# One TensorE-bound kernel, one core: the constants' tiles allocated in another order

## The chip, the core and the metric

The kernel runs on one core of one Trainium2 chip. The time is device microseconds of one execution; the median of three runs counts. A core has TensorE (PE in the profile, its weight loads apart as PEld), VectorE (DVE), ScalarE (ACT), GpSimd (POOL) and SyncE (SP), which here issues all transfers. All tiles of SBUF have an address in bytes within a partition; "at a multiple of 256" below is said of that address.

## What is computed

Two layers of an encoder on 256 frames of 1,024 channels in float32. Each layer normalises its input, projects it by one wide matrix, lets three token mixers work on slices of the projection, merges them by gates, and adds an output projection to its input. Cut to what matters here:

```python
for l in range(DEPTH):                       # 2
    h = _rms(x, norm_g[l])                   # 256 x 1024
    proj = h @ w_in[l]                       # 1024 x 9304
    (gq, gk, gv, ga, gz, bq, bk, bv, iq, ik, iw, bz,
     cq, ck, cv, cz, gate) = jnp.split(proj, SPLIT_AT, axis=-1)
    ...
    merged = (g[:, :, 0] * (y_a @ w_br[l, 0])
              + g[:, :, 1] * (y_b @ w_br[l, 1])
              + g[:, :, 2] * (y_c @ w_br[l, 2]))
    x = x + merged @ w_out[l]
```

## The kernel before

Every float32 operand of a large product is split into a rounded high part and the rest, and a product is three matmuls: high by high, high by low, low by high. `mm3` issues them (lines 183, 184 and 185), so each line of the profile with one of these numbers is one of the three. Each matmul loads its own stationary operand.

The input of a layer is normalised, transposed on TensorE and written by `norm_in` into two tiles, `hTh` (high) and `hTl` (low), each 128 partitions by 8 blocks of channels by 256 frames; line 224 (ACT) writes the high part and line 225 (DVE) the low part. They stay in place for both layers. A slice of them for a block k and a half t of the frames is 128 columns, 512 bytes of each partition, and slices follow each other every 512 bytes.

Weights come in units of 512 KB, laid out on the host in the order of use. For each unit `Stream.need` issues the transfer into a `raw` tile, ACT writes the high part `whi` and DVE the low part `wlo` (line 145). There are 5 `raw` tiles and 6 of each of the others, and units are asked for 21 ahead.

The large matmuls are of three kinds.

- 16 projections of 512 columns in a layer (`bq`, `cq`, `ck`, `cz`, `bk`, `cv`, `gq`, `bv`, `gv`, `gz`, and `gate` six times), through `proj` and `project`. The slice of `hTh` or `hTl` is stationary and 512 columns of `whi` or `wlo` stream past it. A projection has 4 units of 2 blocks, 2 halves and 3 matmuls, so 48 matmuls; in two layers they are 32 x 48 = 1,536.
- `iq` and `bz`, through `project_T`: here 128 columns of the weights are stationary and `hTh[:, k]` or `hTl[:, k]`, 256 columns, stream; 96 matmuls each in a layer, 384 in all. `small_task` has 24 more such in a layer.
- The branch projections `br` and the output projection `out`, again with 512 columns of the weights streaming (at the very end some with 256). Their stationary slices are those of `yTh`, `yTl`, `ybh`, `ybl`, `mTh` and `mTl`, which lie in the pool's tag `kp`.

Between them `Flow.pump` lets smaller tasks issue their matmuls at fixed points of the program; the order of every engine is settled when the program is built, by a scheduler's model, and doesn't depend on the run.

The pool `cp` holds what stays for the whole run. It hands out addresses in the order in which its tiles are asked for: `x` (line 102), `eyeg` (109, the identity and the gains), `half`, `warm` (111, 112), `pk`, `wah`, `wal` (113 to 115), `hTh`, `hTl` (200, 201), and some small ones after these. The pool begins at byte 16,512, which is 128 above a multiple of 256. The pools of the weights and of the work tiles stand behind it: the 17 tiles of the weights' pool begin at 49,152 and all lie at multiples of 4,096, and the tiles of `kp` begin at 138,496 (541 times 256) and are 2,048 bytes each, so their slices of 512 bytes lie at multiples of 256 too.

Of the kernel before, what the change touches and what calls it, by code (L numbers as in the profile page):

```python
# [8 lines left out]
F32 = mybir.dt.float32  # L9
F32R = mybir.dt.float32r  # L10
# [6 lines left out]
L, T, D, BR = 2, 256, 1024, 512  # L17
NB = 3
P = 128
NOSYNC = mybir.DependencyInfo(mybir.DependencyClass.NoSync, mybir.DependencyReason.DATA)  # L20
CH = 512
KD8 = D // P
# [43 lines left out]
def trunk(ctx: ExitStack, tc: tile.TileContext, x_in, units, wsmall, eye, pack, ptmp, wa2b, out):  # L66
# [3 lines left out]
    cp = ctx.enter_context(tc.tile_pool(name="cp", bufs=1))  # L70
# [6 lines left out]
    def nm(s):  # L77
        cnt[0] += 1
        return f"{s}_{cnt[0]}"
# [19 lines left out]
    def at(shape, n="at"):  # L99
        return pp.tile(shape, F32, tag="at", bufs=4, name=nm(n))  # L100

    x = cp.tile([P, 2, D], F32, name="x")
    HV = [slice(h * 512, h * 512 + 512) for h in range(2)]

# [3 lines left out]

    eyeg = cp.tile([P, P + L * KD8], F32, name="eyeg")
    ident, gT = eyeg[:, :P], eyeg[:, P:]  # L110
    half = cp.tile([P, 16], F32, name="half")
    warm = cp.tile([P, 16], F32, name="warm")
    pk = cp.tile([P, NPK], F32, name="pk")
    wah = cp.tile([P, L, 256], F32R, name="wah")
    wal = cp.tile([P, L, 256], F32R, name="wal")
# [77 lines left out]
    def split(ps, shape, n, mk=None):  # L193
# [2 lines left out]
        A.activation(hi, ps, AF.Copy)  # L196
        V.tensor_sub(lo, ps, hi.bitcast(F32))
        return hi, lo

    hTh = cp.tile([P, KD8, T], F32R, name="hTh")  # L200
    hTl = cp.tile([P, KD8, T], F32R, name="hTl")

    ss = [cp.tile([P, 2], F32, name=f"ss{t}") for t in range(2)]

# [731 lines left out]
```

## Time and profile before

| what | value |
|---|---|
| median of three runs | 612.82 us (612.48 to 613.51) |
| the profiled execution | 613.26 us |
| its span, first to last instruction | 611.5 us |
| TensorE busy | 604.2 us, 99% of the span |
| VectorE, ScalarE, GpSimd busy | 434.1, 354.0, 63.0 us |
| mean granted clock of TensorE | 0.994 of full speed |
| read from memory | 99.23 MB, 164 GB/s over the span |

A page of the profile gives the busy time of each engine, the chain of work that ended last, and groups of instructions with their number and the mean length of one. Matmuls are pipelined and their ends are modelled, so in a stream their lengths overlap and are not what they cost. What a matmul costs in a stream is the distance from its start to the start of the next, called its pitch below; the timeline, with starts in hundredths of a microsecond, gives it, best as a mean over a long run.

### The profile page before, as it was taken

To read this page: it belongs to the slowest core of one execution; us is meant where nothing else is said; L and a number is where in the kernel's file an instruction comes from. 1 tells how busy PE (TensorE), PEld (TensorE's weight loads), DVE (VectorE), ACT (ScalarE), POOL (GpSimd) and SP (SyncE) were. 2 spreads that over 40 slices of the span, in tenths; PEclk is the share of its full clock that TensorE was granted. 3 is DMA by queue.
4 is the path that set the end of the run, shared out by engine and by line. 5 is a ranking of instruction groups with operands and counts; after the bars stand their busy time and mean duration, and the time that the engine had idled before them with its cause. 6 is when DMAs were issued, how large, how long until landed. Compare 5 with 4: busy or idle time off the path is not lost.

```text
span 611.5 us, 8711 instructions
## 1 busy us (share of the span) xinstructions
PE 604.2 (99%) x3180; PEld 507.3 (83%) x3180; DVE 434.1 (71%) x709; ACT 354.0 (58%) x612; POOL 63.0 (10%) x93
## 2 busy tenths in 40 slices
PE   7999999999999999999999999999999999999997
PEld 4788888898899888888878888889888988888886
DVE  5888657777989756648587776676888976575571
ACT  6778855766536754443466787576755555544430
POOL 2033101000022000000001340201000120000000
PEclk7999999999999999999999999999999999999999
DMA  8764565425534635555527455533554165455501
GB/s 319 279 208 138 173 206 173 138 104 173 173 103 167 190 129 198 177 194 181 172 87 244 152 161 183 195 115 104 184 167 166 48 230 158 152 177 201 178 30 70
DMA packets 28699, 100.85 MB, mean 165 GB/s; under 512 B 3184, under 2 KB 3696, under 8 KB 28656
## 3 DMA queue, kind: packets, MB, share of 16 engines
q1 hardware_dynamic: 28656, 100.30, 49.6%
q8 instruction: 25, 0.41, 0.3%
q14 instruction: 18, 0.15, 0.1%
HBM read 99.23 MB, written 1.05 MB: 164 GB/s over the span
## 4 chain that ended last, share of the span: by engine, by line
PE 97%; ACT 1%; DMA 1%; DVE 0%; SPq 0%; issue 0%
PE gate L183 7%; PE gate L184 7%; PE gate L185 7%; PE br L183 4%; PE br L184 4%; PE br L185 4%; PE out L185 2%; PE out L183 2%; PE out L184 2%; PE bz L185 1%; PE bz L183 1%; PE cq L183 1%; PE bz L184 1%; PE iq L183 1%; PE iq L185 1%; PE iq L184 1%
## 5 line engine op out<-in xcount | busy, mean ns | idle before, releaser
L145 DVE TENSOR_TENSOR wlo<-raw,whi 128x1024 fp32r<-128x1024 f32 x184 | 224.1, 1222 | 100.1 <-ACT whi L145 98.8
L145 ACT ACTIVATE whi<-raw 128x1024 fp32r<-128x1024 f32 x184 | 193.8, 1060 | 148.6 <-PE gate L185 39.6
L183 PE MATMUL gate<-whi,hTh 128*128 128x512 f32 x192 | 76.6, 399 | 0.0
L184 PE MATMUL gate<-wlo,hTh 128*128 128x512 f32 x192 | 76.1, 396 | 0.0
L185 PE MATMUL gate<-whi,hTl 128*128 128x512 f32 x192 | 75.9, 395 | 0.0
L185 PEld LDWEIGHTS gate<-whi,hTl 128*128 128x128 f32 x192 | 36.1, 188 | 8.1
L183 PEld LDWEIGHTS gate<-whi,hTh 128*128 128x128 f32 x192 | 36.1, 188 | 7.8
L184 PEld LDWEIGHTS gate<-wlo,hTh 128*128 128x128 f32 x192 | 36.2, 188 | 7.7
L190 POOL TENSOR_TENSOR r<-v,half 128x4 f32<-128x4 f32 (+1 forms) x24 | 34.2, 1424 | 2.0
L189 POOL TENSOR_SCALAR v<-ss 128x4 f32<-128x4 f32 (+1 forms) x24 | 11.8, 490 | 182.3 <-DVE ss L268 111.0
L183 PE MATMUL out<-whi,mTh 128*128 128x512 f32 (+1 forms) x72 | 26.7, 371 | 0.0
L184 PE MATMUL out<-wlo,mTh 128*128 128x512 f32 (+1 forms) x72 | 26.3, 366 | 0.0
L185 PE MATMUL out<-whi,mTl 128*128 128x512 f32 (+1 forms) x72 | 26.2, 366 | 0.0
L184 PE MATMUL br<-wlo,yTh 128*128 128x512 f32 x64 | 25.0, 390 | 0.0
L183 PE MATMUL br<-whi,yTh 128*128 128x512 f32 x64 | 25.0, 390 | 0.0
L185 PE MATMUL br<-whi,yTl 128*128 128x512 f32 x64 | 24.9, 389 | 0.0
L183 PE MATMUL iq<-hTh,whi 128*128 128x256 f32 x64 | 18.5, 289 | 0.0
L185 PE MATMUL bz<-hTh,wlo 128*128 128x256 f32 x64 | 18.2, 285 | 0.0
L184 PE MATMUL iq<-hTl,whi 128*128 128x256 f32 x64 | 18.2, 284 | 0.0
L183 PE MATMUL bz<-hTh,whi 128*128 128x256 f32 x64 | 18.1, 283 | 0.0
L184 PE MATMUL bz<-hTl,whi 128*128 128x256 f32 x64 | 18.0, 282 | 0.0
L185 PE MATMUL iq<-hTh,wlo 128*128 128x256 f32 x64 | 18.0, 281 | 0.0
(320 smaller groups left out, 1511.1 us busy)
## 6 DMA issues: line engine op xcount, KB each, us to landing
raw<-in_units SPq DMA_DIRECT2D x184, 512.0 KB, 3.4
x<-in_x SPq DMA_DIRECT2D x4, 256.0 KB, 4.5
wsr<-in_wsmall SPq DMA_DIRECT2D x2, 416.0 KB, 6.3
out<-x SPq DMA_DIRECT2D x3, 256.0 KB, 2.0
pt<-in_ptmp SPq DMA_DIRECT2D x1, 384.0 KB, 7.3
wa<-in_wa2b SPq DMA_DIRECT2D x1, 256.0 KB, 7.3
out<-x SPq DMA_DIRECT2D x2, 128.0 KB, 1.7
pk<-in_pack SPq DMA_DIRECT2D x1, 133.0 KB, 7.6
```

The lines of the kernel that those rows point to most:

```text
L145: self.splits.append((A.activation(hi, raw, AF.Copy), V.tensor_sub(lo, raw, hi.bitcast(F32))))
L183: TE.matmul(ps, lh, rh, start=first, stop=False)
L184: TE.matmul(ps, lh, rl, start=False, stop=False)
L185: TE.matmul(ps, ll, rh, start=False, stop=last)
L189: G.tensor_scalar(v, ss, 1.0 / dim, EPS, op0=OP.mult, op1=OP.add)
L190: G.tensor_tensor(r, v, half[:, :n], op=OP.pow)
```

## The change

The requests for `half`, `warm`, `hTh` and `hTl` are moved ahead of the one for `x`. Nothing else is edited. On each of the five engines the built program has the same instructions in the same order as before. What differs is where nine tiles lie:

| tile | bytes | address before | above a multiple of 256 | address after | above a multiple of 256 |
|---|---|---|---|---|---|
| `hTh` | 8,192 | 30,592 | 128 | 16,640 | 0 |
| `hTl` | 8,192 | 38,784 | 128 | 24,832 | 0 |
| `x` | 8,192 | 16,512 | 128 | 33,024 | 0 |
| `eyeg` | 576 | 24,704 | 128 | 41,216 | 0 |
| `half` | 64 | 25,280 | 192 | 16,512 | 128 |
| `warm` | 64 | 25,344 | 0 | 16,576 | 192 |
| `pk` | 1,064 | 25,408 | 64 | 41,792 | 64 |
| `wah` | 2,048 | 26,496 | 128 | 42,880 | 128 |
| `wal` | 2,048 | 28,544 | 128 | 44,928 | 128 |

All tiles behind these, those of the other pools included, keep their addresses. Slices of 512 bytes of `hTh` and `hTl` lie 384 bytes above a multiple of 512 before, and 256 above one after, as do the slices in `kp`.

```diff
+    half = cp.tile([P, 16], F32, name="half")
+    warm = cp.tile([P, 16], F32, name="warm")
+    hTh = cp.tile([P, KD8, T], F32R, name="hTh")
+    hTl = cp.tile([P, KD8, T], F32R, name="hTl")
     x = cp.tile([P, 2, D], F32, name="x")
...
     eyeg = cp.tile([P, P + L * KD8], F32, name="eyeg")
     ident, gT = eyeg[:, :P], eyeg[:, P:]
-    half = cp.tile([P, 16], F32, name="half")
-    warm = cp.tile([P, 16], F32, name="warm")
     pk = cp.tile([P, NPK], F32, name="pk")
...
-    hTh = cp.tile([P, KD8, T], F32R, name="hTh")
-    hTl = cp.tile([P, KD8, T], F32R, name="hTl")
```

## Rows read from the trace of the kernel before

**Rows 1.** The page, its first part (engine, busy us, share of the span, instructions) and the first line of its fourth (the chain that ended last, by engine).
```profile
PE 604.2 (99%) x3180; PEld 507.3 (83%) x3180; DVE 434.1 (71%) x709; ACT 354.0 (58%) x612; POOL 63.0 (10%) x93
...
PE 97%; ACT 1%; DMA 1%; DVE 0%; SPq 0%; issue 0%
```

**Rows 2.** The waits of TensorE over the whole span: who waited for whom, us in total, times, longest.
```profile
PE bq L183 <- ACT hTh L224: 1.3, 2, 1.1
...
PE cq L183 <- ACT whi L145: 0.3, 1, 0.3
PE bq L184 <- DVE wlo L145: 0.2, 1, 0.2
```

**Rows 3.** Groups of matmuls by line, operands and shape, with their count, busy us and mean ns of one, the idle time before them last.
```profile
L183 PE MATMUL gate<-whi,hTh 128*128 128x512 f32 x192 | 76.6, 399 | 0.0
...
L183 PE MATMUL br<-whi,yTh 128*128 128x512 f32 x64 | 25.0, 390 | 0.0
...
L183 PE MATMUL out<-whi,mTh 128*128 128x512 f32 x56 | 22.1, 394 | 0.0
L183 PE MATMUL iq<-hTh,whi 128*128 128x256 f32 x64 | 18.5, 289 | 0.0
...
L278 PE MATMUL qkT<-eyeg,qn 128*128 128x128 f32 x64 | 9.6, 272 | 0.0
...
L183 PE MATMUL out<-whi,mTh 128*128 128x256 f32 x16 | 4.6, 288 | 0.0
```

**Rows 4.** Groups of weight loads in the same form (the first shape is that of the loaded slice).
```profile
L183 PEld LDWEIGHTS gate<-whi,hTh 128*128 128x128 f32 x192 | 36.1, 188 | 7.8
...
L183 PEld LDWEIGHTS br<-whi,yTh 128*128 128x128 f32 x64 | 12.0, 188 | 2.6
```

**Rows 5.** The timeline of TensorE through the projection `bk` of the first layer, an unbroken run of 48 matmuls: start us, us of one, operands. The last row is the matmul behind the run.
```profile
77.36 0.39 PE L183 MATMUL bk<-whi,hTh 128*128 128x512 f32 x1
77.58 0.39 PE L184 MATMUL bk<-wlo,hTh 128*128 128x512 f32 x1
77.81 0.40 PE L185 MATMUL bk<-whi,hTl 128*128 128x512 f32 x1
78.05 0.40 PE L183 MATMUL bk<-whi,hTh 128*128 128x512 f32 x1
78.29 0.40 PE L184 MATMUL bk<-wlo,hTh 128*128 128x512 f32 x1
...
88.51 0.39 PE L183 MATMUL cv<-whi,hTh 128*128 128x512 f32 x1
```

**Rows 6.** The timeline of TensorE from a run of 60 matmuls of the last `gate` of the first layer (its second is the first row) into the branch products that follow it, 72 of them, and on to `out`. The row of 272.13 is the ninth of the 72.
```profile
256.52 0.39 PE L184 MATMUL gate<-wlo,hTh 128*128 128x512 f32 x1
...
270.05 0.39 PE L185 MATMUL gate<-whi,hTl 128*128 128x512 f32 x1
270.28 0.40 PE L183 MATMUL br<-whi,yTh 128*128 128x512 f32 x1
...
272.13 0.39 PE L185 MATMUL br<-whi,yTl 128*128 128x512 f32 x1
272.36 0.39 PE L183 MATMUL br<-whi,yTh 128*128 128x512 f32 x1
...
286.64 0.39 PE L183 MATMUL out<-whi,mTh 128*128 128x512 f32 x1
```

**Rows 7.** The timeline of TensorE at `out` of the first layer, from four transposes through the 60 matmuls behind them; the row of 297.10 is the seventh of the 60, the last row the sixtieth.
```profile
295.27 0.60 PE L761 MATMUL mT<-eyeg,m 128*128 128x128 f32 x4
295.63 0.48 PE L183 MATMUL out<-whi,mTh 128*128 128x512 f32 x1
295.94 0.39 PE L184 MATMUL out<-wlo,mTh 128*128 128x512 f32 x1
...
297.10 0.39 PE L183 MATMUL out<-whi,mTh 128*128 128x512 f32 x1
...
309.11 0.39 PE L185 MATMUL out<-whi,mTl 128*128 128x512 f32 x1
```

**Rows 8.** The timeline of TensorE through `iq` of the first layer, 57 matmuls of 256 columns without a break.
```profile
123.65 0.28 PE L184 MATMUL iq<-hTl,whi 128*128 128x256 f32 x1
...
130.30 0.28 PE L183 MATMUL iq<-hTh,whi 128*128 128x256 f32 x1
```

**Rows 9.** The timeline of TensorE at the end of the program, the 24 matmuls of `out` of 256 columns.
```profile
605.31 0.28 PE L183 MATMUL out<-whi,mTh 128*128 128x256 f32 x1
...
608.07 0.28 PE L185 MATMUL out<-whi,mTl 128*128 128x256 f32 x1
```

**Rows 10.** The timeline of TensorE: the first and the last of the 81 places at which a matmul of 512 columns with `hTh` or `hTl` stationary is followed by a matmul of another kind.
```profile
13.37 1.83 PE L220 MATMUL hps<-eyeg,h 128*128 128x128 f32 x8
...
568.82 0.40 PE L183 MATMUL br<-whi,yTh 128*128 128x512 f32 x1
```

**Rows 11.** The page, its fifth part: the split of the weights, on DVE and on ACT, 184 units (busy us, mean ns of one, idle time before them and who ended most of it).
```profile
L145 DVE TENSOR_TENSOR wlo<-raw,whi 128x1024 fp32r<-128x1024 f32 x184 | 224.1, 1222 | 100.1 <-ACT whi L145 98.8
L145 ACT ACTIVATE whi<-raw 128x1024 fp32r<-128x1024 f32 x184 | 193.8, 1060 | 148.6 <-PE gate L185 39.6
```

**Rows 12.** Two stretches: us from the span's start, length, busy us of PE, PEld, DVE, ACT and POOL with instructions, granted clock, busy share of the DMA engines, GB/s.
```profile
15.00:40.00 25.00, 24.72 (x123) 20.24 (x122) 21.03 (x44) 19.09 (x36) 2.42 (x4) 1.00 0.78 264
77.36:88.40 11.04, 11.04 (x49) 8.97 (x48) 6.19 (x6) 5.35 (x7) 0.00 (x0) 1.00 0.67 218
```

## Prediction

> **What bounds the kernel now.** I read the page first, then the waits of TensorE, then its timeline. TensorE is busy for 604.2 of 611.5 us, and 97% of the chain that ended last is its own work [rows 1]. It hardly waits: the largest wait for another engine is 1.3 us over the whole run, the next ones 0.3 and 0.2 [rows 2]. So the time is the sum of the pitches of some 3,180 matmuls, and a change that touches no instruction can gain or lose only through a pitch. In the groups the matmuls of one shape are not equally long: 399 ns for `gate`, 390 for `br`, 394 for `out`, all with 512 columns [rows 3]. These lengths are modelled, so I turn to starts.
>
> Through `bk`, whose stationary operand is `hTh` or `hTl`, 48 pitches take from 77.36 to 88.51: 11.15 us / 48 = 232.3 ns. The first of them are 220, 230, 240 and 240 ns to the hundredth [rows 5], so the pitch moves about and does not settle. In the last `gate`, with the same operands, 59 pitches from 256.52 to 270.28 give 233.2 ns [rows 6]. The branch products follow it with nothing in between. Their first 8 pitches, 270.28 to 272.13, still average 231.2 ns; the other 64, to 286.64, take 14.51 us, or 226.7 ns [rows 6]. `out` does the same after an interruption: 5 pitches of 232 ns from 295.94 to 297.10, then 53 from there to 309.11 at 226.6 ns [rows 7]. Moving operand, shape, weights' buffers, traffic and clock are of the same kind on both sides. What differs is the stationary tile: `hTh` and `hTl` lie 128 bytes above a multiple of 256, those of `br` and `out` on one.
>
> The excess can't be a weight load that visibly takes longer: the mean load is 188 ns in both kinds [rows 4]. What the profile has is a correlation of the settled pitch with the stationary tile, at about 5.9 ns, and nothing that names the cause.
>
> **The change part by part.** *The instructions* stay, in number and order, on every engine; nothing is removed, added or queued elsewhere, so no wait changes its place.
>
> *The 1,536 matmuls with `hTh` or `hTl` stationary* get slices with the same place above a multiple of 512 (256) as those of `br` and `out`. If the address is what sets the pitch, theirs goes from about 232.5 ns, between the two runs above and nearer to `bk`, to 226.7, that is 5.8 to 5.9 ns less. Not all 1,536 take part. At 81 places a run of them is broken by other work [rows 10], and the pitch behind a transpose (295.63 to 295.94, 310 ns, [rows 7]) is set by the break; some 10 at the start run at half clock. That leaves about 1,440: 1,440 x 5.9 = 8.5 us. But a run does not settle at once. In aligned tiles the pitch was 231 to 232 ns for 5 to 8 matmuls behind a break [rows 6, 7]. Charged once for each of 81 runs this takes back 5 x 5.3 = 27 ns to 8 x 4.5 = 36 ns each, 2.1 to 2.9 us in all (many runs are shorter than 8, so the upper end is too dear). The gain is 5.6 to 6.4 us, and I take **6.0 us**. Without any settling cost it would be 8.5; with 12 matmuls to settle in each run (81 x 12 x 4.5 ns = 4.4) it would be about 4.
>
> *The 432 matmuls with `hTh` or `hTl` streaming* (`iq`, `bz`, the small task) have a pitch of 6.65 us / 56 = 118.8 ns over `iq` [rows 8]. The one settled run of 256 columns with both operands on multiples of 256 stands at the end of `out`, 2.76 us / 23 = 120.0 ns [rows 9]. By that row these would lose 432 x 1.2 = 0.5 us; by the same size the other way they would gain as much. I take nothing, and keep +-0.5 us for the range. So too for the transposes, which stream the identity out of `eyeg`: a per cent of their largest group, 9.6 us [rows 3], is 0.1 us.
>
> *`x`, `half`, `warm`, `pk`, `wah`, `wal`* are read and written by DVE, ACT, POOL and the transfers, none of which TensorE waits for beyond the 1.3 us named [rows 2]. I cost them at nothing. The cover is the slack of those engines. Where it is thinnest, from 15 to 40 us, DVE is busy 21.03 of 25.00 us and ACT 19.09 [rows 12], and a TensorE that runs 2.5% faster there may meet some tenths of a microsecond of waiting for a split unit (1.06 us on ACT, then 1.22 us on DVE for each, [rows 11]). In `bk` DVE has 6.19 of 11.04 us [rows 12], so there is room.
>
> The profiled execution took 613.26 us, 0.44 above the median; from it the sum gives 607.3, and against the median of 612.82 it is **606.8 us**.
>
> **A rule that speaks against it.** The trace shows two settled pitches for one shape, 232.3 and 226.7 ns [rows 5, 6]. The Trainium skill, page "SBUF — State Buffer", section "Specifications (TRN2)", gives SBUF lines of 16 bytes, with a penalty where accesses cross to a new line too often; 128 bytes above a multiple of 256 is on such a line already, so by it the move is worth nothing. The page "TensorE: Matmul & The Clock Gate", section "Back-to-back issue gap", gives a gap of N / 2.4 + 2.5 ns, 215.8 for 512 columns, with no address in it; neither run here agrees with it. By these two pages the sum would be 612.8, the first rival below.
>
> **The rivals.**
>
> *Nothing changes (612.8 us).* The pitch goes with something else in which `hT` differs from the tiles of `br` and `out`: its region (16 to 47 KB, ahead of the weights, before and after, against 138 KB and up), its place in the program, or what runs beside it. For it: `iq` loads its stationary slices from the weights' tiles, which lie on multiples of 256, streams from `hT`, and its mean is not the 120.0 of `out` either [rows 8, 9], so a stationary tile on such a multiple isn't enough for that pitch. Against it: the switch to 226.7 comes within 8 matmuls of the change of stationary tile, with no break and no other change [rows 6]. The two pages above stand with this rival.
>
> *Partly (about 610 us).* The runs with `hT` settle late or at a pitch between the two, say 230.5 ns: 1,440 x 2 = 2.9 us.
>
> *Slower (614.3 us).* The unsettled pitch has two forms, 232.3 in `bk` and 233.2 in `gate` [rows 5, 6], so it seems to lock to some phase between loading and streaming. The new addresses could lock it to the worse one everywhere: 1,440 x 0.7 = 1.0 us, and `iq` and `bz` to 120.0 for another 0.5. It decides from a settled pitch above 232.5 ns. If each pitch became like the 240 ns seen singly in `bk`, it would be 1,440 x 7.5 = 11 us, but no run holds that.
>
> **How the numbers follow.** The forecast, settled pitch 226.7 with the cost of settling: 0.66, from 604.1 (8.5 us and the 0.5 of the streaming ones the lucky way would be 603.8; I cut a little) to 608.8 (slow settling). Partly: 0.10, 608.8 to 611.5. Nothing: 0.15, 612.2 to 613.4. Slower: 0.09, 614 and more. Two runs of this kernel can hardly be told apart below 0.2%, 1.2 us. Faster by more than that holds the first two, 0.76; within 0.2% the third, 0.15; slower 0.09. For 8 in 10 the range takes the first two cases and about half of the third: 604.1 to 612.9.
>
> **What would show it.** In the profile after, the 48 pitches of `bk` should take about 48 x 226.7 = 10.9 us instead of 11.15, `gate` in the groups should show about 390 ns instead of 399, and the mean of `br` and `out` should stay. Pitches of 226.7 with the total unchanged would mean a new wait, which the waits of TensorE must then show behind L145. A `bk` that still takes 11.15 us makes the address innocent and the prediction wrong; a gain of 8 us or more would say that settling costs nothing behind a break; `iq` at 120.0 or below 118 says what the streaming operand's address does.

## The result and the profile after

The changed kernel takes 606.52 us (median of 5 runs, 605.53 to 607.09) against 612.82 us before: a ratio of 0.9901, 95% interval 0.9890 to 0.9911, or 6.3 us. The profiled execution took 607.09 us with a span of 605.3, against 613.26 and 611.5.

The page after: TensorE's busy time fell by 604.2 - 598.0 = 6.2 us, as much as the span, and its share of the chain is what it was [rows 1].

```profile
PE 598.0 (99%) x3180; PEld 506.9 (84%) x3180; DVE 433.8 (72%) x709; ACT 354.0 (58%) x612; POOL 63.7 (11%) x93
...
PE 97%; DMA 1%; ACT 1%; DVE 0%; SPq 0%; issue 0%
```

The timeline through `bk` of the first layer (the last row is the matmul behind the run of 48):

```profile
76.81 0.39 PE L185 MATMUL bk<-whi,hTh 128*128 128x512 f32 x1
77.04 0.39 PE L186 MATMUL bk<-wlo,hTh 128*128 128x512 f32 x1
77.27 0.39 PE L187 MATMUL bk<-whi,hTl 128*128 128x512 f32 x1
77.50 0.39 PE L185 MATMUL bk<-whi,hTh 128*128 128x512 f32 x1
...
87.69 0.39 PE L185 MATMUL cv<-whi,hTh 128*128 128x512 f32 x1
```

The starts are now 230 or 220 ns apart, and the 48 pitches take 87.69 - 76.81 = 10.88 us, 226.7 ns each, where they took 11.15 [rows 5]. The run from the last `gate` of the first layer (its second matmul first) into the branch products and on to `out`:

```profile
253.98 0.39 PE L186 MATMUL gate<-wlo,hTh 128*128 128x512 f32 x1
...
267.15 0.39 PE L187 MATMUL gate<-whi,hTl 128*128 128x512 f32 x1
267.38 0.39 PE L185 MATMUL br<-whi,yTh 128*128 128x512 f32 x1
...
283.69 0.39 PE L185 MATMUL out<-whi,mTh 128*128 128x512 f32 x1
```

59 pitches of `gate` take 13.40 us, 227.1 ns with the settling at its start, against 233.2; the 72 pitches of `br` take 16.31 us, 226.5 ns from the first one on. Before, they needed 8 matmuls to settle behind `gate` [rows 6]; now there is nothing to settle from.

The groups by form show the same in the modelled lengths: `gate` 394 instead of 399 ns, `br` at 389 instead of 390 [rows 3]. The prediction's sign for `gate` was about 390. The group's mean still holds 17 matmuls that stand first behind a break, with some 441 ns in both traces; the 129 that come tenth or later in a run went from 395 to 389.

```profile
L185 PE MATMUL gate<-whi,hTh 128*128 128x512 f32 x192 | 75.7, 394 | 0.0
...
L185 PE MATMUL br<-whi,yTh 128*128 128x512 f32 x64 | 24.9, 389 | 0.0
...
L185 PE MATMUL iq<-hTh,whi 128*128 128x256 f32 x64 | 18.6, 290 | 0.0
```

`iq` got a little longer (290 against 289 ns). Its timeline, 57 matmuls of 256 columns without a break:

```profile
122.48 0.28 PE L186 MATMUL iq<-hTl,whi 128*128 128x256 f32 x1
...
129.18 0.28 PE L185 MATMUL iq<-hTh,whi 128*128 128x256 f32 x1
```

6.70 us / 56 = 119.6 ns, where it was 118.8 [rows 8]. The waits of TensorE are those of before [rows 2]; no new one took the place of what went:

```profile
PE bq L185 <- ACT hTh L223: 1.4, 2, 1.2
...
PE cq L185 <- ACT whi L147: 0.3, 1, 0.3
PE bq L186 <- DVE wlo L147: 0.2, 1, 0.2
```

Over the whole trace there are 1,404 pitches between neighbouring matmuls of 512 columns with `hT` stationary that no break lengthens (below 245 ns; the same count in both traces). Their mean was 232.5 ns and is 228.1. They form 80 runs. In the changed kernel the first three pitches of a run average 231 to 233 ns, and from the tenth on the mean is 226.7; before, it is 232.3 to 232.8 at the start of a run and further on alike.

### The profile page after: what moved, and what is told of

Its sections match the earlier page's. It is cut to its first block, busy times and chain, and to the rows that moved or that the text cites. A ratio compares the mean times of both kernels' runs of the same rounds, so it can differ in the third digit from the quotient of the medians.

```text
span 605.3 us, 8711 instructions
## 1 busy us (share of the span) xinstructions
PE 598.0 (99%) x3180; PEld 506.9 (84%) x3180; DVE 433.8 (72%) x709; ACT 354.0 (58%) x612; POOL 63.7 (11%) x93
## 4 chain that ended last, share of the span: by engine, by line
PE 97%; DMA 1%; ACT 1%; DVE 0%; SPq 0%; issue 0%
PE gate L185 7%; PE gate L187 7%; PE gate L186 7%; PE br L187 4%; PE br L186 4%; PE br L185 4%; PE out L187 2%; PE out L185 2%; PE out L186 2%; PE bz L187 1%; PE bz L185 1%; PE iq L185 1%; PE iq L186 1%; PE iq L187 1%; PE bz L186 1%; PE cq L185 1%
```

## Experiments

All times are medians with the ratio to the kernel before on the same chip. "Distance" is the address of the stationary slice minus that of the streaming operand, modulo 256. In the first four kernels I thought only of the stationary address; the weights stood on multiples of 256 in all of them, so there the two are the same.

**In place.** `half` and `warm` go behind `hTl` in the old order, which lowers `hTh` and `hTl` (`hT` below) by 128 bytes, and `pk`, `wah` and `wal` with them, and leaves `x` and `eyeg` where they were.

```diff
-    half = cp.tile([P, 16], F32, name="half")
-    warm = cp.tile([P, 16], F32, name="warm")
     pk = cp.tile([P, NPK], F32, name="pk")
...
     hTl = cp.tile([P, KD8, T], F32R, name="hTl")
+    half = cp.tile([P, 16], F32, name="half")
+    warm = cp.tile([P, 16], F32, name="warm")
```

> hTh and hTl stay in their old region, 128 bytes lower, and so on a multiple of 256 (30,464 and 38,656); x and eyeg stay 128 bytes above one. If the address of the stationary operand within 256 bytes is the cause: 606.5 us, bk in 10.9 us, settled pitch 226.7 ns. If the region is the cause: 612.8 us and 11.15 us. If x or eyeg carry part of the gain: in between.

606.36 us, 0.9905 (0.9887 to 0.9922). `bk` takes 10.88 us, 226.7 ns a pitch, and the mean of the 1,402 pitches is 228.1 ns:

```profile
75.45 0.39 PE L181 MATMUL bk<-whi,hTh 128*128 128x512 f32 x1
...
86.33 0.39 PE L181 MATMUL cv<-whi,hTh 128*128 128x512 f32 x1
```

The whole gain comes without `x` and `eyeg` and in the old region.

**`x` and `eyeg` alone.** `half` and `warm` go ahead of `x`, which puts `x` and `eyeg` 128 bytes higher; `hT` and all other tiles stay where they were.

> Only x and eyeg are put on multiples of 256 (16,640 and 24,832); hTh and hTl keep their old addresses, 128 above one. If the stationary operand is the cause: 612.8 us, pitches of bk still 232 ns. If x and eyeg, which the transfers, VectorE, ScalarE and the transposes use, carry the gain: 606.5 us.

613.04 us, 1.0006 (0.9997 to 1.0015); mean pitch 232.7 ns. These two tiles carry nothing.

**The new region, 128 off.** The changed kernel with `half` and `warm` behind `hTl`.

```diff
-    half = cp.tile([P, 16], F32, name="half")
-    warm = cp.tile([P, 16], F32, name="warm")
     hTh = cp.tile([P, KD8, T], F32R, name="hTh")
     hTl = cp.tile([P, KD8, T], F32R, name="hTl")
+    half = cp.tile([P, 16], F32, name="half")
+    warm = cp.tile([P, 16], F32, name="warm")
```

> The order of the changed kernel but for half and warm, which go behind hTl: hTh and hTl in the new region at 16,512 and 24,704, 128 above a multiple of 256; every other large tile where the changed kernel has it. Stationary address as the cause: 612.8 us, pitch 232 to 233 ns. Region or the neighbours as the cause: 606.5 us.

612.79 us, 1.0004 (0.9995 to 1.0014). `bk` in its timeline:

```profile
76.99 0.40 PE L185 MATMUL bk<-whi,hTh 128*128 128x512 f32 x1
77.23 0.39 PE L186 MATMUL bk<-wlo,hTh 128*128 128x512 f32 x1
77.46 0.40 PE L187 MATMUL bk<-whi,hTl 128*128 128x512 f32 x1
...
88.19 0.40 PE L185 MATMUL cv<-whi,hTh 128*128 128x512 f32 x1
```

48 pitches in 11.20 us, 233.3 ns: the worse of the two forms, with `bk` alternating between some 238 and 229 ns where it took the better one before [rows 5]. The total didn't move for it, since other runs went the other way. The region is out as a cause, and so is the slower rival. `x`, `eyeg`, `pk`, `wah` and `wal` stand here where the changed kernel has them, and carry nothing.

**64 off a multiple of 128.** `hTh` and `hTl` stand between `half` and `warm`, at 192 above a multiple of 256.

> hTh and hTl 192 bytes above a multiple of 256 (16,576 and 24,768), so 64 above one of 128. If only multiples of 256 settle: the pitch is 231 ns or more, 612 to 615 us. If what counts is how many lines of 256 bytes a slice of 512 touches, the same as at 128: 612.8 us. If it counts in steps of 64: 606.5 us.

607.70 us, 0.992 (0.9906 to 0.9935), which none of the three expectations had. `bk`, and then `iq`:

```profile
76.76 0.39 PE L185 MATMUL bk<-whi,hTh 128*128 128x512 f32 x1
...
87.74 0.39 PE L185 MATMUL cv<-whi,hTh 128*128 128x512 f32 x1
```

```profile
122.45 0.28 PE L186 MATMUL iq<-hTl,whi 128*128 128x256 f32 x1
...
128.82 0.28 PE L185 MATMUL iq<-hTh,whi 128*128 128x256 f32 x1
```

`bk` takes 10.98 us / 48 = 228.8 ns, between the two levels known so far, and `iq`, where `hT` streams, 6.37 us / 56 = 113.8 ns, less than in any kernel ahead of it (its distance is 64 here, the weights being the stationary side). So there are more than two levels, and 256 columns have their own best place. With 1,404 pitches at a mean of 229.55 instead of 228.10 ns (2.0 us dearer) and 354 in `iq` and `bz` at 115.7 instead of 119.5 (1.3 cheaper), this kernel should lie 0.7 us above the changed one. The two traces that these means are from differ by 605.9 - 605.3 = 0.6 us in span; by the medians it is 1.2.

**A multiple of 512.** `negi` is taken ahead of `hTh` too, so that `hT` starts on a multiple of 512 instead of 256 above one.

> hTh and hTl on multiples of 512 (16,896 and 25,088) instead of 256 above one; x, eyeg and the weights' and work pools as in the changed kernel. If the place within 256 bytes is all that counts: 606.5 us, settled pitch 226.7 ns. If the slices must lie 256 above a multiple of 512, as those in kp do: 608 us or more.

606.22 us, 0.9892 (0.9875 to 0.9908), mean pitch 228.1 ns. The place within 256 bytes is all that counts; in the first kernel of matmuls below, distances of 256, 320, 384 and 448 repeat the pitches of 0, 64, 128 and 192.

**The mirror.** An unused tile of 128 bytes ahead of the tag `kp` in the changed kernel shifts the stationary tiles of `br` and `out`.

```diff
+        if l == 0:
+            sp.tile([P, 32], F32, tag="pad", bufs=1, name="pad")
         bqT = [(kp([P, 4, P], F32R, "bqh"), kp([P, 4, P], F32R, "bql")) for _ in range(2)]
```

> The changed kernel with the tag kp and all tags behind it moved up by 128 bytes: now the stationary slices of br and out lie 128 above a multiple of 256 and hT lies on one. If the stationary address is the cause, br and out (448 matmuls of 512 columns) lose the settled 226.7 ns and stand at 232 to 233 ns, 448 x 5.8 ns = 2.6 us: 609.1 us, with the projections unchanged. If the projections' gain came from anything else: 606.5 us.

609.11 us, 0.9943 (0.9927 to 0.9958), as the stationary address has it, and the distance too, since the weights stayed on multiples of 256. The timeline from the last `gate` into `br` and on to `out`:

```profile
267.53 0.40 PE L187 MATMUL gate<-whi,hTl 128*128 128x512 f32 x1
267.76 0.40 PE L185 MATMUL br<-whi,yTh 128*128 128x512 f32 x1
...
284.50 0.39 PE L185 MATMUL out<-whi,mTh 128*128 128x512 f32 x1
```

72 pitches in 16.74 us, 232.5 ns, against 226.5, while the projections keep a mean of 228.1.

**Everything 128 off.** The kernel before with 128 unused bytes behind its last constant, so that the weights' and work tiles go where `hT` already is within 256 bytes.

```diff
     nlam = cp.tile([P, L], F32, name="nlam")
+    cp.tile([P, 32], F32, name="pad")
```

> The kernel before with 128 unused bytes behind its last constant: hTh, hTl keep their addresses, 128 above a multiple of 256, and all weights' and work tiles move up by 128, so that they lie 128 above one too. No large operand is on a multiple of 256. If what counts is the distance between the stationary and the streaming operand, modulo 256: all distances are 0, settled pitch 226.7 ns in projections, br and out, 606.4 us. If what counts is the stationary tile's own address: 232 to 233 ns in all 1,984 matmuls of 512 columns, 615 us.

606.53 us, 0.9899 (0.9884 to 0.9914), the time of the changed kernel with no large operand on a multiple of 256. `bk`:

```profile
76.51 0.39 PE L183 MATMUL bk<-whi,hTh 128*128 128x512 f32 x1
...
87.39 0.39 PE L183 MATMUL cv<-whi,hTh 128*128 128x512 f32 x1
```

10.88 us / 48 = 226.7 ns. This decides it: the distance counts, not the multiple.

**The cost by itself.** Two kernels of matmuls alone, on four tiles: once these are loaded, no other engine works beside TensorE.

> Leaves out the whole model (the output is the input): 43 runs of 48 matmuls in the manner of the projections on four tiles, each run with its own place of the stationary slices and of the streaming operand within 256 bytes, TensorE alone. If the stationary address sets the pitch by itself, also without other engines: 226.7 ns at 0 and 256, 232 to 233 at 128 and 384, 229 at 64 and 192 below a streaming operand at 0. If it is the distance between the two operands: stationary 128 with streaming 128 gives 226.7 again. If traffic of other engines has part in it: 226.7 everywhere. 256 columns streaming: 120 ns at 0, 113.3 at 192, 118.8 at 128.

> Leaves out the model as the first such kernel did: 40 runs of 48 matmuls. 512 columns: if only a distance of 0 settles well, every distance from 8 to 252 gives 228 to 234 ns; a distance with less than 226.7 would be a better place for hT. 256 columns: 120 at 0, 113.4 at 64 whatever the addresses; if the state also depends on what ran before, equal distances in different order (64 over 0, 0 over 192) differ, 113.4 against 117.8 ns.

First the run of the first kernel in which the streaming operand stands at 64 and the stationary one at 0, 64, 128 and 192 (each row is the first matmul of a run of 48, of 512 columns; the names hold the two places):

```profile
238.54 0.39 PE L103 MATMUL s0m64n512t0x<-Wh,Sh 128*128 128x512 f32 x1
...
249.53 0.39 PE L103 MATMUL s64m64n512t0x<-Wh,Sh 128*128 128x512 f32 x1
...
260.42 0.40 PE L103 MATMUL s128m64n512t0x<-Wh,Sh 128*128 128x512 f32 x1
...
271.62 0.39 PE L103 MATMUL s192m64n512t0x<-Wh,Sh 128*128 128x512 f32 x1
...
282.77 0.39 PE L103 MATMUL s0m128n512t0x<-Wh,Sh 128*128 128x512 f32 x1
```

The differences of the rows over 48 are 229.0, 226.9, 233.3 and 232.3 ns, for distances 192, 0, 64 and 128. Four distances at four places of the streaming operand repeat these levels. Means of pitches 17 to 47 of the runs of 512 columns:

| distance | 0 | 4 | 8 | 16 | 32 | 64 | 96 | 128 | 160 | 176 | 192 | 208 | 224 | 240 | 248 | 252 |
|---|---|---|---|---|---|---|---|---|---|---|---|---|---|---|---|---|
| ns | 226.7 | 232.5 | 230.7 | 233.3 | 233.4 | 233.4 | 234.4 | 232.5 | 233.4 | 230.0 | 228.9 | 231.9 | 233.3 | 226.7 | 233.4 | 226.7 |

The other seven tried (48, 80, 112, 144, 184, 200, 216) lie between 230.7 and 233.4. No distance tried goes below 226.7, so `hT` has no better place among them for the projections; but 240 and 252 share the level of 0, against the expectation of 228 to 234 everywhere else. Engines beside it aren't needed for it: the levels of the model's own runs come back with TensorE alone. What the chip does in these 6 ns isn't shown by any of this; the levels are settled patterns, and 248 between 240 and 252 warns against reading a smooth law into them.

With 256 columns a distance doesn't fix the level. In the first kernel, stationary 0 and streaming 192 gives 117.8 ns, where 113.3 had been expected from the kernel with `hT` 64 off. Five runs of the second kernel, in order (the place of the stationary and of the streaming operand in the name, first matmul of each run of 48):

```profile
257.19 0.28 PE L100 MATMUL c30s0m64n256t0x<-Wh,Sh 128*128 128x256 f32 x1
...
262.63 0.28 PE L100 MATMUL c31s0m192n256t0x<-Wh,Sh 128*128 128x256 f32 x1
...
268.29 0.28 PE L100 MATMUL c32s64m0n256t0x<-Wh,Sh 128*128 128x256 f32 x1
...
273.94 0.29 PE L100 MATMUL c33s0m192n256t0x<-Wh,Sh 128*128 128x256 f32 x1
...
279.40 0.28 PE L100 MATMUL c34s128m64n256t0x<-Wh,Sh 128*128 128x256 f32 x1
```

Differences over 48: 113.3, 117.9, 117.7 and 113.8 ns. The second and the fourth run have the same addresses, stationary 0 and streaming 192, and stand at 117.9 and 113.8 (113.3 once settled). They write different accumulators, but the third run, stationary 64 and streaming 0 at 117.7, has its counterpart with the same operands and the same two accumulators in the first kernel:

```profile
416.80 0.28 PE L103 MATMUL s64m0n256t0x<-Wh,Sh 128*128 128x256 f32 x1
...
422.26 0.28 PE L103 MATMUL s128m0n256t0x<-Wh,Sh 128*128 128x256 f32 x1
```

5.46 us / 48 = 113.8 ns, 113.3 once settled. What is left between the two is what ran before, so that has part in it. At distance 0 all runs settle at 120.

**A version from it.** 64 bytes between stationary weights and streaming `hT` in `iq` and `bz`, with the projections left at 0. The split tiles are widened by 256 bytes; to pay for them there are 4 `raw` tiles, which also moves some instructions.

```diff
-                hi = wp.tile([P, 1024], F32R, tag="whi", bufs=BUFS["wt"], name=nm("whi"))
-                lo = wp.tile([P, 1024], F32R, tag="wlo", bufs=BUFS["wt"], name=nm("wlo"))
+                hi = wp.tile([P, 1088], F32R, tag="whi", bufs=BUFS["wt"], name=nm("whi"))
+                lo = wp.tile([P, 1088], F32R, tag="wlo", bufs=BUFS["wt"], name=nm("wlo"))
+                a = SHIFT if j % NUNIT in STATIONARY else 0
+                hi, lo = hi[:, a:a + 1024], lo[:, a:a + 1024]
...
+SHIFT = 16
+STATIONARY = {UNIT[c] + i for c in ("iq", "bz") for i in range(4)}
...
-BUFS = dict(w2=6, kp=25, w4=6, ev=2, raw=5, wt=6, ahead=21)
+BUFS = dict(w2=6, kp=25, w4=6, ev=2, raw=4, wt=6, ahead=21)
```

> The changed kernel with tiles of the split weights widened by 256 bytes, the parts of iq and bz written 64 bytes into them, and 4 raw tiles instead of 5 to pay for the room (which also moves some instructions). If the distance is the cause, stationary 64 above streaming gives iq and bz 113.4 ns instead of 120, 354 x 6 ns = 2.1 us: 604.3 us, the projections unchanged at 226.7. If 4 raw tiles are too few, waits for whi or wlo take it back: 606.5 us or more.

604.91 us, 0.9876 (0.9859 to 0.9892), 0.6 us above what was expected. The control has the same tiles, buffers and order and a shift of 0, and the shifted kernel ran once more beside it.

> The shifted kernel with a shift of 0: widened weight tiles and 4 raw tiles, iq and bz at distance 0 again. If the shift carries the gain: iq and bz at 120 ns and about 2 us slower than the shifted kernel, 606.5 to 607. If the 4 raw tiles or the moved instructions carry it: the same 604.9 us.

> The shifted kernel once more beside its control, on the same chip: 604.9 us, 113.4 ns in most of iq and bz; about 2 us below the control.

Control 607.24 us, 0.9914 (0.9901 to 0.9928); shifted 605.28 us, 0.9887 (0.9873 to 0.9900). `iq` in the shifted kernel, then in the control:

```profile
123.07 0.28 PE L192 MATMUL iq<-hTl,whi 128*128 128x256 f32 x1
...
129.43 0.28 PE L191 MATMUL iq<-hTh,whi 128*128 128x256 f32 x1
```

```profile
123.50 0.28 PE L192 MATMUL iq<-hTl,whi 128*128 128x256 f32 x1
...
130.20 0.28 PE L191 MATMUL iq<-hTh,whi 128*128 128x256 f32 x1
```

6.36 us / 56 = 113.6 ns against 119.6. In `iq` and `bz` together 354 pitches have a mean of 114.25 instead of 119.49 ns, 1.9 us, and the times differ by 1.96. The shifted kernel is the fastest of all; its lead over the changed one, 1.2 to 1.6 us by the medians, wasn't timed side by side and the intervals still touch (0.9900 and 0.9890). The control shows why it isn't the full 2 us: 607.24 against 606.52, some 0.7 us lost with 4 `raw` tiles and the moved instructions, a difference that the intervals (0.9901 to 0.9928 and 0.9890 to 0.9911) don't secure.

## Why the prediction was right, and where its reason was too narrow

- **What bounds the kernel.** Right: the time went where the pitches went. TensorE's busy time and the span both fell by 6.2 us, and no wait grew.
- **The projections' 8.5 us.** Right in mechanism, a little dear in size: the trace has 1,404 unlengthened pitches instead of 1,440, and 1,404 x (232.5 - 226.7) = 8.1 us.
- **The settling, 2.1 to 2.9 us.** Measured: 1,404 x (228.1 - 226.7) = 2.0 us over the 80 runs, and the first eight pitches of the runs hold 1.9 of it. A gain of 8 us would have needed it to vanish. The forecast charged 0.1 to 0.9 us too much here and counted 0.4 us too much gain on the line above. That its 6.0 us came so close owes something to these two errors going against each other.
- **The streaming operand, nothing taken, 0.5 us at the ends.** Measured: 354 x (119.5 - 118.7) = 0.3 us lost, on the side that the run of `out` [rows 9] had shown.
- **Not in the sum:** `br` needs no settling behind `gate` any more. The mean of `br` and `out` over 445 pitches went from 227.2 to 226.9, 0.2 us won. Together: 8.1 - 2.0 - 0.3 + 0.2 = 6.0 of the 6.2 us of the span.
- **`x`, `eyeg` and the small tiles at nothing.** Right: 1.0006 with `x` and `eyeg` moved alone. With all large tiles but `hT` in their new places, `pk`, `wah` and `wal` among them, it is 1.0004. `half` and `warm` took no experiment of their own; they moved in both of these kernels and left no mark.
- **The cause.** The prediction put it in the stationary tile's own address, "hTh and hTl lie 128 bytes above a multiple of 256, those of br and out on one". That step was too narrow, though the sum didn't hang on it: it counted the streaming operand as the same on both sides, which it was, and so could not see that its address belongs to the rule. With everything 128 off, the address is the bad one and the pitch the good one. In this kernel both readings give the same time, since the weights stood on multiples of 256.
- **Rival "nothing changes".** The region fell by two kernels (old region, new distance: fast; new region, old distance: slow). Its argument from `iq` is explained: `iq` had the same distance of 128, from the other side. The lines of 16 bytes on the Trainium skill's page "SBUF — State Buffer", section "Specifications (TRN2)", don't give it either: 16 bytes of distance cost 233.3 - 226.7 = 6.6 ns a matmul, and 4 bytes 232.5 - 226.7 = 5.8.
- **Rival "partly".** A level between the two exists, 228.9 at distance 192, but it is a settled one and not slow settling.
- **Rival "slower".** Its two forms are real: `bk` takes the one of 233.3 ns in the kernel with `hT` in the new region, 128 off, and the one of 232.3 before, at the same distance. It takes 233.3 (76.38 to 87.58 us) with `x` and `eyeg` moved alone too, where `hT` and the weights have the very addresses of before. But the runs swap the forms, and the total stays within 0.1%. The prediction called these pitches unsettled, and there it misread [rows 5]: in the trace's starts, which are whole ns, `bk` before repeats a cycle of seven pitches (228, 230, 233, 241, 232, 231, 232, to 1 ns) to its end, the form of 233.3 is a cycle of two, and that of 226.7 one of three (227, 227, 226).

## What to carry to other kernels

Where TensorE is the bound and float32 matmuls follow each other, measure the pitch (start to start in the timeline) of a long run and compare it between groups of one shape; the mean length in the groups shows only part of it. If two groups differ, look at where their two operands lie modulo 256 bytes, relative to each other: 128 bytes more or less in a pool shift all tiles behind them against those ahead, and here that cost 1%. Put the pair of the most frequent matmul at distance 0, and try other distances for other shapes, with 256 columns above all. All runs here had float32 operands in the form that the kernel splits them into and 128 stationary columns; other types weren't tried.

## What the runs showed of the chip that was not expected

- The pitch of a float32 matmul with its own weight load depends on the distance of its operands in SBUF modulo 256 bytes: 226.7 ns for 512 columns at distance 0 (and 240 and 252) and 229 to 234 at the others tried, with TensorE alone as in the full kernel. The Trainium skill, page "TensorE: Matmul & The Clock Gate", section "Back-to-back issue gap", has no address in its figures: N / 2.4 + 2.5 ns for a matmul by itself, 215.8 for 512 columns, and about 131 ns for one in a stream of weight loads and matmuls. No run here reached either; the shortest single pitch of 512 columns in any trace is 223 ns.
- With 256 columns the order turns: 120 ns at distance 0, and 113.3 at 64 or 192 in some runs (117.8 in others).
- The levels are states that a stream settles into, within some 10 matmuls in the projections (231 to 233 ns at first, 226.7 from the tenth pitch on), and the same addresses can hold two of them: 117.8 and 113.3 ns for 256 columns, by what ran before, and 232.3 and 233.3 for 512 in `bk`, where the reason isn't shown.
